# Gate matmuls of a recurrent layer: from two block-diagonal weights over the whole array to one head per half of the array's rows

## The chip, the cores and the metric

The kernel runs on one core of one Trainium2 chip. The metric is the device time of one execution in microseconds (us), lowest is best. TensorE (PE in the profile) does the matmuls, VectorE (DVE) and ScalarE (ACT) the elementwise work, GpSimd (POOL) and SyncE (SP) mostly issue DMAs.

## The reference, cut to what matters

One pre-norm layer over 2048 prompt positions and 128 sample positions (8 streams of 16), model width 1024. RMSNorm, one input projection, two branches (S5 and RG-LRU), a gated merge, an output projection, a final RMSNorm. The change is in the RG-LRU branch, whose two gates are block-diagonal: 16 heads of 64 channels, each with its own 64x64 weight per gate.

```python
xc, conv_new = causal_conv(u_b, conv_buf, conv_w, conv_b)
xh = xc.reshape(bt, L, LRU_HEADS, LRU_HEAD_DIM)            # 16 heads of 64
r = sigmoid(einsum('blhi,hij->blhj', xh, wa) + ba)         # recurrence gate
i = sigmoid(einsum('blhi,hij->blhj', xh, wx) + bx)         # input gate
log_a = -8.0 * r * softplus(-lam)
a = exp(log_a)
g = sqrt(max(-expm1(2 * log_a), 0)) * (i * xc)
h_t = a_t * h_{t-1} + g_t
y_b = h * silu(z_b);  p_b = y_b @ w_pb
```

## The kernel before, in words

Channels lie on the 128 partitions and positions along the free dimension. The 2176 positions are cut into five tiles `n`: four of 512 columns and one of 128. The 1024 recurrent channels are cut into eight blocks `b` of 128 channels, so a block holds two heads of 64.

Every fp32 product is made of three fp16 passes: weight and data are each split into a high and a low half, and the passes are high x high, high x low, low x high (`gemm`). A projection (`proj`) of one block and tile is 8 x 3 = 24 such matmuls.

The stage of the change is "stage B", a loop over `b`. It has an order written out by hand, and each engine runs its instructions in that order:

1. For each `n`: PE does the projection of the branch input (`proj`), and from `n` = 2 on the gate matmuls of tile `n-2` (`gates_pe`). ACT copies the projection out (`ub`), DVE does the width-4 convolution into `xc` (four instructions), ACT applies the two Tanh of the gates of `n-2` (`gates_a`, tiles `pt` and `q`), ACT rounds `xc` to the fp16 high half (`conv_hi`, tile `xs`), ACT does Exp and Tanh of `gates_b`, DVE makes the low half (`conv_lo`), DVE multiplies (`gates_c`).
2. `split_bd` splits the next block's gate weights (tile `wbs`).
3. For `n` = 0 and 1: the projection of the branch's SiLU gate, with the gate matmuls of tiles 3 and 4 behind it, then `gates_a`, `silu_tile` (tile `sz`), `gates_b`, `gates_c` of these.
4. The next streamed weight is split on ACT and DVE (`ws.step`, tile `wsp`). ACT loads the table for Sqrt and does `root_tile` for all five tiles; DVE then does product, scan and output product for each tile (`scan_tile`, `y_hi`, `y_lo`), while ACT goes back to the Tanh table for the last three `silu_tile`.

PSUM has four buffers `mm` for the projections and two each of `a` and `b` for the gates, 512 fp32 columns each. A projection can start only when the one four back has been read. After stage B comes stage P4B (gate B, projection B, and the S5 branch interleaved in it), where the same four `mm` buffers go round.

Before the change one block's weights are `[128, gate, 128]`: for each gate a 128x128 matrix with the two heads' 64x64 blocks on its diagonal and zeros elsewhere. `gates_pe` issues three 128x128 matmuls of 512 columns for the recurrence gate into buffer `a`, then three for the input gate into `b`; the output rows are the 128 channels in order, so one Tanh of 128 partitions evacuates each gate.

Of the kernel before, what the change touches and what calls it, by code (L numbers as in the profile page):

```python
# [17 lines left out]
P = 128  # L18
D = 1024
# [10 lines left out]
# column starts of the combined input projection  # L30
C_UA, C_ZA, C_UB, C_ZB, C_GA, C_GB = 0, 512, 1024, 2048, 3072, 4096

# power-of-two scales of the fp16 (high, low) parts
# [9 lines left out]
# per-pair parameter record of the S5 branch (float32 words per partition)  # L43
# [5 lines left out]
def build(tc, I, O):  # L49
# [30 lines left out]
    with ExitStack() as es:  # L80
# [45 lines left out]
        class Stream:  # L126
# [18 lines left out]
            def step(self):  # L145
                """splits the next block and starts the load two further on."""
                while self.nl < min(self.ns + 2, len(self.jobs)):
                    self.load()
                self.split()
                while self.nl < min(self.ns + 2, len(self.jobs)):  # L150
                    self.load()
# [6 lines left out]
        def rstd(r, ss, t):  # L158
            """r = -2 / sqrt(ss / D + eps): the table's root, then one Newton step."""
            act(r, ss, AF.Sqrt, scale=1.0 / D, bias=epsb)  # L160
            ts(t, ss, 1.0 / D, EPS, MUL, ADD)
            V.reciprocal(out=r, in_=r)
            if r.shape[1] == 1:
                stt(t, r, t, r, MUL, MUL)
            else:
                tt(t, t, r, MUL)
                tt(t, t, r, MUL)
            stt(r, t, -3.0, r, ADD, MUL)
# [3 lines left out]
        def gemm(p, W, rhs, nk):  # L172
            """p += the three passes of (Wh + Wl)^T (xh + xl) over nk blocks of the contraction."""
            for k in range(nk):
                xh, xl = rhs(k)
                PE.matmul(p, lhsT=W[:, k, 0], rhs=xh, start=(k == 0), stop=False)  # L176
                PE.matmul(p, lhsT=W[:, k, 0], rhs=xl, start=False, stop=False)  # L177
                PE.matmul(p, lhsT=W[:, k, 1], rhs=xh, start=False, stop=(k == nk - 1))  # L178
# [11 lines left out]
        wbdt = cp.tile([P, 2, 2, P], F32, name="wbd")  # L190
        G.memset(wbdt, 0.0)
        wbd = [wbdt[:, i] for i in range(2)]

        def load_bd(b):
            r = wbd[b % 2]
            for i, k in enumerate(("lru_wa", "lru_wx")):
                for h in range(2):
                    SP.dma_start(out=r[64 * h:64 * h + 64, i, 64 * h:64 * h + 64], in_=I[k][0, 2 * b + h])
# [27 lines left out]
        # =====================================================================  # L226
        # RMSNorm of the input, its transpose, and the S5 input projection
        # =====================================================================
# [5 lines left out]
        with ExitStack() as p1x:  # L234
# [84 lines left out]
            def params():  # L319
# [37 lines left out]
                def gma(out, a, f, b):  # L357
                    """out = f * a + b"""
                    gts(out, a, f)
                    gtt(out, out, b, ADD)  # L360

                def pexp(out, x):
                    """exp by range reduction and a polynomial."""
                    n, r, a, t = nt(), nt(), nt(), nt()
                    gts(x, x, -87.0, 88.0, MAX, MIN)
                    gts(n, x, 1.0 / math.log(2.0), MAGIC, MUL, ADD)
                    gts(n, n, -MAGIC, op0=ADD)
                    gma(t, n, -0.693359375, x)
                    gma(r, n, 2.12194440e-4, t)
                    G.memset(a, 1.0 / 5040)  # L370
                    for f in (720, 120, 24, 6, 2, 1, 1):
                        gtt(a, a, r, MUL)
                        gts(a, a, 1.0 / f, op0=ADD)
                    gts(n, n, 127.0, 8388608.0, ADD, MUL)
                    G.tensor_copy(out=r.bitcast(I32), in_=n)
                    gtt(out, a, r, MUL)
# [10 lines left out]
                def reduce_(a, k):  # L387
                    """a minus its nearest multiple of two pi."""
# [39 lines left out]
                # lambda_bar and the input coefficient (lambda_bar - 1) / lambda  # L428
# [11 lines left out]
                # lambda_bar^16 in polar form  # L440
                gtt(l16[:, 0], m16, cs[:, 1], MUL)
                gtt(l16[:, 1], m16, sn[:, 1], MUL)
                # parameters stacked by (re, im) over the partitions, one column per group
# [26 lines left out]
                # B_bar = coefficient * B, and i * B_bar  # L470
# [9 lines left out]
                # phasors exp(i 16 theta c), c = 0..127  # L480
# [73 lines left out]
            # the first tile: transposed as its rows arrive, all eight banks at once  # L554
# [68 lines left out]
        # =====================================================================  # L623
        # generic slots for everything that follows
        # =====================================================================
# [14 lines left out]
        # recurrent and convolution states, tails of both  # L640
# [24 lines left out]
        def split_bd(b):  # L665
            w = gt([P, 2, 2, P], F16, name="wbs")
            wsplit(w, wbd[b % 2], 2)
            wbs[b] = w
# [4 lines left out]
        def conv_tile(b, n, p):  # L673
            """evacuates the projection, applies the causal convolution, splits the result."""
# [36 lines left out]
        def gates_pe(b, n):  # L711
            w = TILES[n][1]
            xc, xs = st[b, n]
            out = []
            for i, tag in enumerate("ab"):
                p = ps(tag)[:, :w]
                gemm(p, wbs[b][:, i:i + 1], lambda k: (xs[:, 0], xs[:, 1]), 1)
                out.append(p)
            return out

        def gates_a(b, n, pr, pi):
            xc = st[b, n][0]
            pt, q = wt(n, name="pt"), wt(n, name="q")
            act(pt, pr, AF.Tanh, scale=0.5 / WS, bias=HB[:, b:b + 1])
            act(q, pi, AF.Tanh, scale=0.5 / WS, bias=HB[:, 8 + b:9 + b])
# [155 lines left out]
        def s5_mats(q):  # L881
# [9 lines left out]
            # wb[j, g, h, t] = lambda^(15 - 8j - t) B_bar, wc[j, g, h, t] = C lambda^(8j + t + 1)  # L891
# [21 lines left out]
        def s5_pe1(q):  # L913
# [10 lines left out]
            # lag kernels K[0..15] of both groups  # L924
# [147 lines left out]
        def out_states2():  # L1072
            # S5: lambda_bar^16 h0 + v for the samples, the last chunk state for the prompt
# [304 lines left out]
```

## Time and profile before

| | |
|---|---|
| time, median of 3 timed runs | 1560.04 us (1558.78 to 1561.81) |
| span of the profiled execution, first to last instruction | 1562.1 us |
| the profiled execution's own time | no other than its span; the span lies 2.1 us above the median |
| instructions | 22054 |
| PE busy | 1509.9 us, 97% of the span |
| DVE busy | 886.2 us, 57% |
| ACT busy | 632.9 us, 41% |
| TensorE clock granted, mean | 0.995 of full |

A busy PE is not a PE at its peak: a matmul's record lasts until its results are out, so records overlap. The distance from one start to the next is the pace. The same holds for ACT and DVE records, whose ends overlap the next start a little.

### The profile page before, as it was taken

The page shows a single profiled execution, that of the slowest core. Times are in us where ns is not written, and L with a number is a line of the kernel's source. Part 1 is how long each engine was busy: PE and PEld are TensorE (multiplying, and loading weights), DVE is VectorE, ACT ScalarE, POOL GpSimd, SP SyncE. Part 2 cuts the span into 40 slices and gives each one's busy share as a digit, 9 for nine tenths or more (in the row PEclk, how much of TensorE's full clock was granted, in tenths as well). Part 3 has the DMA queues.
Part 4 walks back from the last instruction along what each step waited for, and adds up shares of the span by engine and source line. Part 5 has one row for each costly group of instructions (what it writes and reads, how often), then busy time and mean ns, then how long its engine had stood idle before and what let it go on. Part 6 is the DMA issues. An engine that isn't in the chain of part 4 may idle for free.

```text
span 1562.1 us, 22054 instructions
## 1 busy us (share of the span) xinstructions
PE 1509.9 (97%) x8552; PEld 759.2 (49%) x8552; DVE 886.2 (57%) x1841; ACT 632.9 (41%) x1204; POOL 170.5 (11%) x344
## 2 busy tenths in 40 slices
PE   7999999999999999999999999979999999999998
PEld 4544444444444445555555554435444444444444
DVE  6557688878888775566655411864623320473333
ACT  7544465456545624444444311742322221242222
POOL 0780000000000003122222210000000000220000
PEclk9999999999999999999999999989999999999999
DMA  8298010101000123323333222231211210352331
GB/s 205 92 98 198 14 29 16 29 14 29 16 27 14 41 71 91 100 84 89 104 90 105 61 62 70 78 103 50 91 50 49 78 49 14 109 168 94 108 108 68
DMA packets 133458, 115.99 MB, mean 74 GB/s; under 512 B 35146, under 2 KB 112602, under 8 KB 132840
## 3 DMA queue, kind: packets, MB, share of 16 engines
q1 hardware_dynamic: 126056, 95.65, 23.4%
q0 software_dynamic: 7296, 18.92, 3.8%
q8 instruction: 67, 1.10, 0.3%
q14 instruction: 39, 0.32, 0.1%
HBM read 83.01 MB, written 31.53 MB: 73 GB/s over the span
## 4 chain that ended last, share of the span: by engine, by line
PE 68%; DVE 18%; ACT 8%; issue 2%; DMA 2%; POOL 1%; SPq 0%; POOLq 0%; DVEq 0%; ACTq 0%
PE ps_mm L176 17%; PE ps_mm L177 17%; PE ps_mm L178 17%; PE ps_mm L1333 4%; PE ps_mm L1334 4%; PE ps_mm L1332 4%; DVE xc L66 3%; DVE q L752 2%; ACT L75 1%; DVE sz L54 1%; ACT yh L75 1%; DVE q L54 1%; DVE wo L66 1%; ACT wsp L75 1%; PE ps_a L932 1%
## 5 line engine op out<-in xcount | busy, mean ns | idle before, releaser
L176 PE MATMUL ps_mm<-hT,wsp 128*128 128x512 f16 (+1 forms) x1440 | 486.2, 347 | 2.2 <-DVE qz L66 1.9
L177 PE MATMUL ps_mm<-hT,wsp 128*128 128x512 f16 (+1 forms) x1440 | 486.7, 347 | 0.0
L178 PE MATMUL ps_mm<-hT,wsp 128*128 128x512 f16 (+1 forms) x1440 | 485.7, 347 | 0.0
L177 PEld LDWEIGHTS <-wsp 128*128 128x128 f16 x2000 | 195.9, 98 | 198.6 <-issue 14.6
L176 PEld LDWEIGHTS <-wsp 128*128 128x128 f16 x2000 | 195.9, 98 | 191.6 <-issue 6.5
L178 PEld LDWEIGHTS <-wsp 128*128 128x128 f16 x2000 | 195.9, 98 | 189.5 <-issue 1.1
L66 DVE SCALAR_TENSOR_TENSOR wsp<-wraw,wsp 128x1024 f16<-128x1024 f32 (+1 forms) x56 | 62.0, 1108 | 111.2 <-ACT wsp L75 110.5
L176 PE MATMUL ps_mm<-y,wsp 128*128 128x512 f16 (+1 forms) x320 | 108.2, 347 | 0.0
L178 PE MATMUL ps_mm<-y,wsp 128*128 128x512 f16 (+1 forms) x320 | 108.2, 347 | 0.0
L177 PE MATMUL ps_mm<-y,wsp 128*128 128x512 f16 (+1 forms) x320 | 108.2, 347 | 0.0
L1333 PE MATMUL ps_mm<-wo,m 128*128 128x512 f16 (+2 forms) x280 | 104.1, 373 | 0.2 <-DVE wo L66 0.2
L1332 PE MATMUL ps_mm<-wo,m 128*128 128x512 f16 (+2 forms) x280 | 104.1, 373 | 0.0
L1334 PE MATMUL ps_mm<-wo,m 128*128 128x512 f16 (+2 forms) x280 | 104.0, 373 | 0.0
L1125 POOL DMA_DIRECT2D mbD<-gb x40 | 22.0, 551 | 663.6 <-DVE gb L66 663.5
L66 DVE SCALAR_TENSOR_TENSOR xc<-ub,PC,xc 128x512 f32<-128x512 f32 (+1 forms) x120 | 80.6, 672 | 4.2
L75 ACT ACTIVATE ga<-ps_mm 128x512 f32<-128x512 f32 (+1 forms) x40 | 21.2, 532 | 123.5 <-PE ps_mm L178 123.5
L75 ACT ACTIVATE gb<-ps_mm 128x512 f32<-128x512 f32 (+1 forms) x40 | 21.2, 530 | 121.0 <-PE ps_mm L178 90.8
L66 DVE SCALAR_TENSOR_TENSOR ga<-ga,ps_mm 128x512 f32<-128x512 f32 (+1 forms) x40 | 24.1, 602 | 79.2 <-PE ps_mm L178 78.8
L75 ACT ACTIVATE jk<-xo 128x512 f16<-128x512 f32 (+2 forms) x35 | 21.6, 617 | 109.5 <-DVE xo L66 109.5
L66 DVE SCALAR_TENSOR_TENSOR xo<-ps_mm,xo 128x512 f32<-128x512 f32 (+2 forms) x35 | 23.6, 675 | 71.0 <-PE ps_mm L1334 71.0
L75 ACT ACTIVATE y<-sz 128x512 f16<-128x512 f32 (+1 forms) x40 | 22.6, 566 | 94.3 <-DVE sz L54 94.3
L75 ACT ACTIVATE xs<-xc 128x512 f16<-128x512 f32 (+1 forms) x40 | 22.6, 566 | 90.7 <-DVE xc L66 90.7
(260 smaller groups left out, 2345.1 us busy)
## 6 DMA issues: line engine op xcount, KB each, us to landing
wraw<-w_in SPq DMA_DIRECT2D x40, 512.0 KB, 4.0
xt<-x_prompt SPq DMA_DIRECT2D x16, 512.0 KB, 4.2
mbD<-gb POOLq DMA_DIRECT2D x32, 256.0 KB, 2.3
ya<-yDp SPq DMA_DIRECT2D x32, 256.0 KB, 4.5
mb<-mbD SPq DMA_DIRECT2D x32, 256.0 KB, 4.2
xo<-x_prompt SPq DMA_DIRECT2D x16, 512.0 KB, 4.5
o_y_prompt<-xo SPq DMA_DIRECT2D x16, 512.0 KB, 2.9
uD<-uE POOLq DMA_DIRECT2D x4, 1088.0 KB, 11.4
```

Source lines behind the costliest of these rows:

```text
L54: V.tensor_tensor(out=out, in0=a, in1=b, op=op)
L66: V.scalar_tensor_tensor(out=out, in0=a, scalar=s, in1=b, op0=op0, op1=op1)
L75: S.activation(out=out, in_=a, func=f, **kw)
L176: PE.matmul(p, lhsT=W[:, k, 0], rhs=xh, start=(k == 0), stop=False)
L177: PE.matmul(p, lhsT=W[:, k, 0], rhs=xl, start=False, stop=False)
L178: PE.matmul(p, lhsT=W[:, k, 1], rhs=xh, start=False, stop=(k == nk - 1))
L752: V.tensor_tensor_scan(out=q, data0=a, data1=q, initial=0.0 if n == 0 else prev[:, w - 1:w], op0=MUL, op1=ADD)
L932: PE.matmul(o[:, 16 + P * j:16 + P * j + w], lhsT=lb, rhs=d["wc"][:, j, g].rearrange("p (h t) -> p t h", t=8)[:, 0:w // 16], start=True, s ...
L1125: G.dma_start(out=mbD[m, :, t0:t0 + w], in_=g)
L1332: PE.matmul(p, lhsT=lh[0], rhs=wo[:, k, 0, c], start=(k == 0), stop=False)
L1333: PE.matmul(p, lhsT=lh[0], rhs=wo[:, k, 1, c], start=False, stop=False)
L1334: PE.matmul(p, lhsT=lh[1], rhs=wo[:, k, 0, c], start=False, stop=(k == KB - 1))
```

## The change

The two heads of a block no longer sit on the diagonal of a 128x128 matrix. Head `h` keeps its rows, the partitions `64*h` to `64*h+63`, and its two 64x64 gate blocks lie side by side in the columns; for head 0 the recurrence gate comes first, for head 1 the input gate (`c = 64 * (i ^ h)`). A matmul therefore contracts over 64 rows, yields 128 output rows, and there is one PSUM buffer for each head in place of one for each gate: `a` holds head 0 (recurrence gate in rows 0 to 63, input gate in 64 to 127), `b` holds head 1 (input gate in rows 0 to 63, recurrence gate in 64 to 127). The three passes are issued in turn for the two heads: six matmuls as before, each on half of the array's rows. The zero fill of the weight tile goes away, and the split of the weights handles 128 columns in place of 256. `gates_a` evacuates by halves: four Tanh of 64 partitions in place of two of 128, because each gate's rows now come from both buffers. The rest of the diff removes comments.

```diff
-        wbdt = cp.tile([P, 2, 2, P], F32, name="wbd")
-        G.memset(wbdt, 0.0)
+        wbdt = cp.tile([P, 2, P], F32, name="wbd")
         wbd = [wbdt[:, i] for i in range(2)]
         def load_bd(b):
             r = wbd[b % 2]
             for i, k in enumerate(("lru_wa", "lru_wx")):
                 for h in range(2):
-                    SP.dma_start(out=r[64 * h:64 * h + 64, i, 64 * h:64 * h + 64], in_=I[k][0, 2 * b + h])
+                    c = 64 * (i ^ h)
+                    SP.dma_start(out=r[64 * h:64 * h + 64, c:c + 64], in_=I[k][0, 2 * b + h])
...
         def split_bd(b):
-            w = gt([P, 2, 2, P], F16, name="wbs")
-            wsplit(w, wbd[b % 2], 2)
+            w = gt([P, 2, P], F16, name="wbs")
+            scopy(w[:, 0], wbd[b % 2], WS)
+            stt(w[:, 1], wbd[b % 2], WS, w[:, 0], MUL, SUB)
             wbs[b] = w
...
         def gates_pe(b, n):
             w = TILES[n][1]
             xc, xs = st[b, n]
-            out = []
-            for i, tag in enumerate("ab"):
-                p = ps(tag)[:, :w]
-                gemm(p, wbs[b][:, i:i + 1], lambda k: (xs[:, 0], xs[:, 1]), 1)
-                out.append(p)
+            out = [ps(tag)[:, :w] for tag in "ab"]
+            for i, (l, r) in enumerate(((0, 0), (0, 1), (1, 0))):
+                for h in range(2):
+                    c = slice(64 * h, 64 * h + 64)
+                    PE.matmul(out[h], lhsT=wbs[b][c, l], rhs=xs[c, r], start=(i == 0), stop=(i == 2))
             return out
 
-        def gates_a(b, n, pr, pi):
+        def gates_a(b, n, p0, p1):
             xc = st[b, n][0]
             pt, q = wt(n, name="pt"), wt(n, name="q")
-            act(pt, pr, AF.Tanh, scale=0.5 / WS, bias=HB[:, b:b + 1])
-            act(q, pi, AF.Tanh, scale=0.5 / WS, bias=HB[:, 8 + b:9 + b])
+            lo, hi = slice(0, 64), slice(64, P)
+            for dst, d, src, c, o in ((pt, lo, p0, lo, 0), (pt, hi, p1, hi, 0), (q, lo, p0, hi, 8), (q, hi, p1, lo, 8)):
+                act(dst[d], src[c], AF.Tanh, scale=0.5 / WS, bias=HB[d, o + b:o + b + 1])
             ts(pt, pt, 1.0, 0.0, ADD, MAX)
             st[b, n] = (xc, pt, q)
```

## Rows read from the trace of the kernel before

**Rows 1.** Page, busy us, share of the span, instructions.
```profile
PE 1509.9 (97%) x8552; PEld 759.2 (49%) x8552; DVE 886.2 (57%) x1841; ACT 632.9 (41%) x1204; POOL 170.5 (11%) x344
```

**Rows 2.** Windows: one block of stage B, a part of it, stage P4B.
```profile
core 0: us, PE busy (x) PEld busy (x) DVE busy (x) ACT busy (x) POOL busy (x), PEclk, DMA share, GB/s
399.70:452.10 52.40, 50.26 (x272) 24.18 (x271) 42.85 (x80) 28.69 (x53) 0.00 (x0) 1.00 0.08 22
...
420.60:434.90 14.30, 14.30 (x72) 6.70 (x71) 11.32 (x24) 13.41 (x25) 0.00 (x0) 1.00 0.08 24
...
585.00:920.00 335.00, 335.00 (x2299) 187.04 (x2297) 184.39 (x503) 137.56 (x308) 76.75 (x130) 1.00 0.30 89
```

**Rows 3.** Waits of PE, 125 to 560 us: total, times, longest.
```profile
PE ps_a L176 <- ACT xs L75: 9.2, 14, 0.7
PE ps_a L177 <- DVE xs L54: 5.8, 14, 0.5
```

**Rows 4.** Chain that ended last, block 5: start, us, what.
```profile
415.22 0.38 PE ps_a L177
...
428.32 0.37 ACT pt L75
```

**Rows 5.** Timeline of ACT, block 5 (start, us, instruction, idle before).
```profile
419.25 0.63 ACT L75 ACTIVATE xs<-xc 128x512 f16<-128x512 f32 x1 [1.89 <-DVE xc L66]
...
421.31 0.68 ACT L75 ACTIVATE pt<-ps_a,HB 128x512 f32<-128x512 f32 x1
421.88 0.68 ACT L75 ACTIVATE q<-ps_b,HB 128x512 f32<-128x512 f32 x1
423.07 0.31 ACT L75 ACTIVATE xs<-xc 128x128 f16<-128x128 f32 x1 [0.51 <-DVE xc L66]
...
424.17 0.72 ACT L75 ACTIVATE pt<-pt,SPL 128x512 f32<-128x512 f32 x1
424.80 0.40 ACT L75 ACTIVATE wbs<-wbd 128x256 f16<-128x256 f32 x1
425.10 0.67 ACT L75 ACTIVATE pt<-ps_a,HB 128x512 f32<-128x512 f32 x1
...
427.47 0.72 ACT L75 ACTIVATE pt<-pt,SPL 128x512 f32<-128x512 f32 x1
428.32 0.37 ACT L75 ACTIVATE pt<-ps_a,HB 128x128 f32<-128x128 f32 x1
428.59 0.36 ACT L75 ACTIVATE q<-ps_b,HB 128x128 f32<-128x128 f32 x1
428.84 0.60 ACT L75 ACTIVATE sz<-ps_mm 128x512 f32<-128x512 f32 x1
```

**Rows 6.** Timeline of DVE, block 5: the first scan's product, the third SiLU.
```profile
433.08 0.69 DVE L54 TENSOR_TENSOR q<-q,pt 128x512 f32<-128x512 f32 x1 [0.72 <-ACT pt L75]
...
441.01 0.69 DVE L66 SCALAR_TENSOR_TENSOR sz<-sz,ps_mm 128x512 f32<-128x512 f32 x1 [2.60 <-ACT sz L75]
```

**Rows 7.** Timeline of ACT in P4B: four copies of 64 partitions out of PSUM.
```profile
579.00 1.14 ACT L75 ACTIVATE v<-ps_a 64x136 f32<-64x136 f32 x4 [0.49 <-PE ps_a L965]
```

**Rows 8.** Timeline of ACT, block 0: gates of its last tile.
```profile
166.27 0.37 ACT L75 ACTIVATE pt<-ps_a,HB 128x128 f32<-128x128 f32 x1 [2.81 <-PE ps_a L178]
...
166.78 0.60 ACT L75 ACTIVATE sz<-ps_mm 128x512 f32<-128x512 f32 x1
```

**Rows 9.** Timelines of DVE and PE where stage B ends.
```profile
553.85 0.68 DVE L66 SCALAR_TENSOR_TENSOR sz<-sz,ps_mm 128x512 f32<-128x512 f32 x1
...
555.23 0.38 PE L176 MATMUL ps_mm<-hT,wsp 128*128 128x512 f16 x1
```

**Rows 10.** Timeline of PE: gate matmuls of one tile, back to back.
```profile
415.87 0.38 PE L177 MATMUL ps_b<-xs,wbs 128*128 128x512 f16 x1
416.08 0.38 PE L178 MATMUL ps_b<-xs,wbs 128*128 128x512 f16 x1
```

**Rows 11.** Timeline of PE in P4B: from 32-column to whole-array matmuls.
```profile
571.94 1.03 PE L932 MATMUL ps_a<-wc,par 128*32 128x128 f32 x7
572.90 0.39 PE L176 MATMUL ps_mm<-y,wsp 128*128 128x512 f16 x1
```

## Prediction, on record before the result

> **What bounds the kernel now.** I began with the page: PE is busy for 97% of the span, which invites the sentence "PE is the bound, so PE time saved is time won" [rows 1]. That is an average over stages, so I asked next for windows. In P4B, PE is busy for all of 335 us; in one block of stage B it is busy for 50.26 of 52.40 us, with DVE at 42.85 and ACT at 28.69 [rows 2]. The 2.1 us that are missing in each block have names: PE waits for `xs`, the split convolution output, first for ACT's high half and then for DVE's low half, 15.0 us over the stage [rows 3]. An engine that waits for its followers isn't the bound there, so I read the chain of the stage. In block 5 it enters PE at 415.22 and leaves it at 428.32, to ACT's first Tanh of the last gate tile [rows 4]. That is 13.1 us of PE in a period of 52.4; the other 39 us of each period are DVE and ACT: convolution, split, roots, scans, output products. Only matmuls issued between these two times can shorten a block.
>
> Then the question is what is second there. The timeline of ACT shows it: from 423.07 on ACT runs one instruction after another up to the roots; in the 14.3 us around them it is busy for 13.41 [rows 2, 5]. The Tanh of 428.32 follows a Tanh of 427.47; at the pace that such a one has (424.17 to 424.80, 0.63 us) ACT came free at 428.10 [rows 5]. So PE is ahead of ACT in setting this time by 0.22 us and no more. What starts behind it, the roots, is waited for: DVE's first scan product stood 0.72 us for its root [rows 6].
>
> **The change part by part.** *PE.* Six matmuls of a tile start 0.21 to 0.22 us apart [rows 10]. If the matmuls of two heads run side by side, a 512-column tile saves three of them, 0.65 us. Over 32 such tiles, and 8 of a quarter of the columns, that is 20.8 + 1.3 = 22 us. No row shows two matmuls side by side in the two halves of the rows, so the bounds are 0 and 0.65 us a tile; I take 0.65, since it has little weight below: in a block only two groups lie between the two times of the chain, 1.30 us, and ACT is 0.22 us behind.
>
> A switch of the array's partition may cost something too. The row that is nearest: the seventh 32-column matmul's record ends at 571.94 + 1.03 = 572.97, and the next whole-array matmul starts at 572.90, so no gap is seen at that switch [rows 11]. The sum takes 0. The upper bound is the overlap of two neighbours lost, 0.38 - 0.21 = 0.17 us a switch, two switches a group [rows 10]. The Trainium skill ("TensorEngine Tiling (Array Packing)", Tiling Modes, Key Properties) speaks against the change here: changing the tiling mode drains TensorE. By that rule half of the saving goes, and the time would be 0.7 us longer (the third rival); the rows of the 32-column switch do not bear it out. For the pairing only the skill has a statement ("TensorE: Matmul & The Clock Gate", Part 3): matmuls in different row groups run concurrently; by it the saving is the 0.65 us that I take, and no row here shows it.
>
> *ACT.* Two Tanh become four of half the partitions. Does half the height cost half? The nearest row says no: four copies of 64x136 out of PSUM took 1.14 us, 0.285 us each, while whole-height Tanh of 128 columns start 0.27 us apart (428.32, 428.59) [rows 5, 7]. Time goes by columns. So a half-height Tanh of 512 columns is priced as a whole one, 0.57 us (421.31 to 421.88), and a tile costs 2 x 0.57 = 1.14 us more, the last tile 0.52 us more (428.32 to 428.84 for two) [rows 5]. The bounds are 0 (half height, half price) and this.
>
> How much of it is on the path, in a block like block 5 [rows 5]:
> - tiles 0 and 1: behind them ACT waits for the convolution, 1.89 us and more; 1.14 fits in. 0.
> - tile 2: its second Tanh lets ACT free at 421.88 + 0.57 = 422.45, the next instruction starts at 423.07. 0.62 is hidden, 0.52 us is not.
> - the split of the gate weights has 128 columns less: (0.57 - 0.27) / 3 = 0.10 us less. DVE's half of it is not waited for.
> - tile 3: ACT is back to back. 1.14 us.
> - tile 4: 0.52 us, less the 0.22 us that ACT stood for PE. 0.30 us.
>
> Sum: 0.52 - 0.10 + 1.14 + 0.30 = 1.86 us later at the roots. What is late next: the Sqrt table load, the roots, the first scan, and by the chain all of the scans, the last SiLU and the next block's convolution. Is there slack to take it up? DVE waits 2.60 us for the third SiLU [rows 6], but that SiLU stands behind the return to the Tanh table, which stands behind the second output product of DVE itself; it moves along. So each period grows from 52.4 to 54.3 us.
>
> *The ends.* Block 0 is different: ACT stands 2.81 us for PE before its last gate tile [rows 8], so PE's saving of two groups counts, -1.30 us, and the two extra Tanh cost 0.52: -0.78 us. Blocks 1 to 6 give 6 x 1.86 = 11.2. In block 7 there is no gate weight to split, so 1.96 there: DVE and ACT reach the end of the stage 12.4 us late. PE doesn't wait for all of it: the first matmul that needs their work is the projection at 555.23, which takes the PSUM buffer that DVE finished reading at 553.85 + 0.68 = 554.53; 0.70 us of slack [rows 9]. PE would come there on its own 10.4 - 1.3 = 9.1 us late, so it waits, and leaves stage B 12.4 - 0.7 = 11.7 us late. P4B has PE full [rows 2], so this goes through to the end.
>
> *At nothing:* the weight loads (as many DMAs, a block ahead), the zero fill at the program's start, the HBM traffic, the DVE operations on `pt` and `q` (they wait for the last Tanh, which in tiles 0 and 1 ends before the convolution does).
>
> Sum on the profiled execution: 1562.1 + 11.7 = 1573.8 us. Its span is 2.1 us above the median of the runs shown, so the forecast is 1571.7 us, 0.75% slower. A measurement of this kernel can tell about 0.2%, 3.1 us, from no change.
>
> **The rivals.**
> 1. *PE is the bound all through stage B.* Then 22 us come off: 1538. For it: 97% busy. Against it: the named waits and a chain that is on PE for a quarter of a period [rows 3, 4]. 0.04.
> 2. *Half height, half price on ACT.* Then ACT gains nothing and loses nothing, each block shortens by the 0.22 us of slack and the 0.10 us of the split, block 0 by 1.3, the end by 0.7: 1556, faster. It decides at a pace of about 0.38 us for 64x512: there the extra 4 x 0.38 - 1.14 = 0.38 us a tile, 1.46 times in a block (tiles 3 and 4), just pays for the 0.32 us, and block 0's gain for the rest. Against it: 0.285 us for 136 columns [rows 7]. 0.05.
> 3. *Every switch drains PE* (the rule above). Block 0 keeps 0.62 of its 1.30 us: 1572.4. 0.12.
> 4. *The heads don't run side by side.* The change doesn't do what it says, PE saves nothing, block 0 gives +0.52 in place of -0.78: 1573.0. Nothing in the rows excludes it; it would hardly show in the time. 0.12.
> 5. *The delay is taken up within the block*, in DVE's 2.60 us [rows 6]. Then blocks 1 to 6 give nothing and what stays is -0.78 + 1.96 - 0.70: 1560.5, no change. Against it: both sides of that wait hang on the same chain. 0.07.
>
> **How the numbers follow.** My own case has 0.60, and its time is the forecast. Cases 3 and 4 lie beside it, so slower holds 0.84, no change 0.07, faster 0.09. The range: with a half-height pace of 0.53 to 0.60 us for 0.57, the block's sum moves by -0.4 to +0.3 us, seven times, -2.8 to +2; if tile 2 were hidden too, -3.6 at most; no pairing adds 1.3. I take 1566 to 1577, which leaves out cases 1, 2 and 5, 0.16.
>
> **What the profile after would show.** Four Tanh of 64 partitions in each tile, each near 0.68 us long and 0.57 apart; ACT some 49 us busier by its records (64 x 0.68 + 16 x 0.36). Gate matmuls of 64 rows whose starts come in pairs, or 0.21 us apart if case 4 holds. The period of a block near 54.3 us, the wait of PE for ACT's `xs` at two places in a block grown from 0.7 to about 2 us, the wait of ACT for PE before the last gate tile gone. P4B and all behind it unchanged in length and shifted by 11.7 us. The forecast is wrong if a 64x512 Tanh has a pace well below 0.57 us, or if ACT still waits for PE between tile 3 and the roots; and too low if the longer waits of PE bring its granted clock to the lower level.

## The result, and the profile after

The changed kernel takes 1585.83 us (median of 4 runs, 1585.14 to 1587.13) against 1559.95 us for the kernel before in the same measurement (4 runs, 1558.78 to 1561.81). The ratio is 1.0168, with a 95% interval of 1.0154 to 1.0182: 1.7% slower. The forecast was 1571.7 us, in a range of 1566 to 1577. The direction and the place were right, the size was half of what came.

The page of the changed kernel, in the columns of [rows 1]:

```profile
PE 1508.3 (95%) x8552; PEld 748.6 (47%) x8552; DVE 890.6 (56%) x1841; ACT 687.7 (43%) x1284; POOL 170.6 (11%) x343
```

PE's and DVE's busy times hardly move; ACT has 80 instructions and 54.8 us more. Windows of one block of stage B and of stage P4B, as in [rows 2]:

```profile
391.30:447.23 55.93, 48.81 (x264) 21.98 (x263) 42.91 (x79) 35.52 (x62) 0.00 (x0) 0.97 0.07 21
607.00:942.00 335.00, 334.17 (x2275) 185.75 (x2273) 184.63 (x507) 138.39 (x307) 76.49 (x129) 1.00 0.30 90
```

A block has grown from 52.4 to 55.9 us, DVE's work in it is the same, and ACT has 6.8 us more. P4B is as full as before: it is shifted, not changed. From one Sqrt table load to the next, six periods of the kernel before are 52.41 us on average and the seventh is 52.96. After the change the six are 55.84 to 55.93, 20.75 us longer together, and the seventh is 56.74, 3.78 longer; the first load comes 1.20 us earlier. So the last load comes 20.75 + 3.78 - 1.20 = 23.3 us later, and this is what the spans differ by too (1585.4 and 1562.1).

The timeline of ACT in the changed kernel's block 5 shows where a period grows; it answers to [rows 5] (`sz` is the SiLU's Tanh, `a` the Exp of `gates_b`):

```profile
433.91 0.67 ACT L75 ACTIVATE pt<-ps_a,HB 64x512 f32<-64x512 f32 x1
434.60 0.68 ACT L75 ACTIVATE pt<-ps_b,HB 64x512 f32<-64x512 f32 x1
...
436.71 0.31 ACT L75 ACTIVATE xs<-xc 128x128 f16<-128x128 f32 x1
...
438.50 0.67 ACT L75 ACTIVATE pt<-ps_a,HB 64x512 f32<-64x512 f32 x1
...
440.59 0.68 ACT L75 ACTIVATE q<-ps_b,HB 64x512 f32<-64x512 f32 x1
441.29 0.60 ACT L75 ACTIVATE sz<-ps_mm 128x512 f32<-128x512 f32 x1
441.91 0.72 ACT L75 ACTIVATE a<-pt,SPL 128x512 f32<-128x512 f32 x1
...
443.29 0.35 ACT L75 ACTIVATE pt<-ps_a,HB 64x128 f32<-64x128 f32 x1
...
444.80 0.60 ACT L75 ACTIVATE sz<-ps_mm 128x512 f32<-128x512 f32 x1
```

And the lines of block 5 before the change that the next paragraph needs besides [rows 5]:

```profile
426.24 0.59 ACT L75 ACTIVATE sz<-ps_mm 128x512 f32<-128x512 f32 x1
426.71 0.72 ACT L75 ACTIVATE a<-pt,SPL 128x512 f32<-128x512 f32 x1
...
429.31 0.41 ACT L75 ACTIVATE a<-pt,SPL 128x128 f32<-128x128 f32 x1
```

Read the starts, not the lengths. A record is 0.68 us long before and after, but before the next Tanh started 0.57 us later [rows 5], and here it starts 0.70 us later. The four Tanh of tile 2 take 2.80 us, and the idle 0.51 us in front of `xs` is gone. Slot by slot, the changed kernel against the kernel before: first Tanh of tile 2 to `xs` 2.80 for 1.76, +1.04; `xs` to the Tanh of tile 3 1.79 for 2.03, -0.24; tile 3's Tanh to its `sz` 2.79 for 1.14, +1.65; the Exp behind that `sz` +0.15; from there to tile 4's Tanh -0.23, the wait for PE that is gone; tile 4's Tanh to `sz` 1.51 for 0.52, +0.99; the next Exp +0.16. The sum is 3.5 us, the growth of the period.

PE's side is small. The timeline of PE, one gate tile between two projections, which answers to [rows 10]:

```profile
435.01 0.38 PE L178 MATMUL ps_mm<-hT,wsp 128*128 128x512 f16 x1
435.32 0.39 PE L721 MATMUL ps_a<-xs,wbs 64*128 64x512 f16 x1
435.33 0.39 PE L721 MATMUL ps_b<-xs,wbs 64*128 64x512 f16 x1
...
435.77 0.38 PE L721 MATMUL ps_b<-xs,wbs 64*128 64x512 f16 x1
436.08 0.39 PE L176 MATMUL ps_mm<-hT,wsp 128*128 128x512 f16 x1
```

The two heads of a pair start 0.01 us apart here, so they do run side by side. Each switch between whole and half array shows as a step of 0.31 us where 0.215 is usual, 0.1 us more. From the last projection matmul to the next one it is 1.07 us, where seven steps of 0.215 would be 1.5: 0.44 us saved a tile.

PE's saving turns into longer waits. PE's waits of the changed kernel, 125 to 600 us, against [rows 3]:

```profile
PE ps_mm L176 <- DVE sz L66: 19.6, 13, 2.1
PE ps_a L721 <- ACT xs L75: 15.5, 9, 1.8
```

And the chain of waits in block 5, which was on PE for 13.1 us [rows 4], goes over DVE and ACT alone from 422 to 446 us; a few of its lines (start, us, what):

```profile
431.84 0.63 ACT xs L75
...
434.60 0.68 ACT pt L75
```

### The profile page after: what moved, and what is told of

Its sections match the earlier page's. It is cut to its first block, busy times and chain, and to the rows that moved or that the text cites. A ratio compares the mean times of both kernels' runs of the same rounds, so it can differ in the third digit from the quotient of the medians.

```text
span 1585.4 us, 22133 instructions
## 1 busy us (share of the span) xinstructions
PE 1508.3 (95%) x8552; PEld 748.6 (47%) x8552; DVE 890.6 (56%) x1841; ACT 687.7 (43%) x1284; POOL 170.6 (11%) x343
## 4 chain that ended last, share of the span: by engine, by line
PE 55%; DVE 15%; ACT 13%; issue 2%; DMA 1%; SPq 0%; ACTq 0%; DVEq 0%; POOL 0%
PE ps_mm L176 14%; PE ps_mm L178 13%; PE ps_mm L177 13%; DVE xc L66 4%; PE ps_mm L1337 4%; PE ps_mm L1336 4%; PE ps_mm L1338 4%; ACT pt L75 3%; DVE q L756 2%; ACT q L75 2%; ACT a L75 1%; DVE sz L54 1%; ACT L75 1%; DVE q L54 1%; ACT yh L75 1%
## 5 line engine op out<-in xcount | busy, mean ns | idle before, releaser
L66 DVE SCALAR_TENSOR_TENSOR gb<-gb,ps_mm 128x512 f32<-128x512 f32 (+1 forms) x40 | 24.0, 602 | 62.0 <-PE ps_mm L178 62.0
```

Of the source, the lines that this page charges most:

```text
L66: V.scalar_tensor_tensor(out=out, in0=a, scalar=s, in1=b, op0=op0, op1=op1)
```

## The experiments

The theory was that ACT's four Tanh carry the whole loss, because half-height instructions follow each other at 0.70 us where whole ones do at 0.57, and that the paired matmuls by themselves are a small gain. The rival was that something on TensorE carries it, or part of it: the switches, or the granted clock, which fell from 0.995 to 0.988 over the whole run. Inside the first theory it was open what makes the pace 0.70. Each expectation explains its own letters. The first four and the next four kernels ran on chips where the kernel before took 1564.05 and 1563.54 us, so ratios are compared, each against the kernel before on the same chip.

**1. The paired matmuls with two Tanh.** After's matmuls; `gates_a` applies two Tanh of 128 partitions, one to each head's buffer, which mixes up the rows of the two gates.

```diff
-            lo, hi = slice(0, 64), slice(64, P)
-            for dst, d, src, c, o in (...):
-                act(dst[d], src[c], AF.Tanh, scale=0.5 / WS, bias=HB[d, o + b:o + b + 1])
+            act(pt, p0, AF.Tanh, scale=0.5 / WS, bias=HB[:, b:b + 1])
+            act(q, p1, AF.Tanh, scale=0.5 / WS, bias=HB[:, 8 + b:9 + b])
```

> The matmul half of the change alone: pairs of 64-row matmuls as in the changed kernel, but two whole-height Tanh as before (pt from head 0's buffer, q from head 1's, so the rows of the two gates are mixed up and the output is not the reference's; the work per engine is what is wanted). Theory A (all of the loss is ScalarE's four Tanh, matmul pairing is harmless and nearly worthless): ACT loses its extra 2 x 0.57 us a tile, each block gives back the 0.22 us for which ACT stood for PE and the 0.10 us of the smaller weight split, block 0 about 1 us: 1556 us (1554 to 1559). Theory B (half-array matmuls cost something: switches of the array, a clock that falls, PSUM buffers given back late): 1565 us or more, with a block's period above 53 us. Theory C (PE is the bound of the stage, and pairing is worth its 0.4 us a tile or more): 1545 us or less.

Measured: 1565.46 us, ratio 1.0013 (1.0003 to 1.0023). The loss is gone, but the gain isn't there. The windows of three of its blocks say why (granted clock: third number from the end):

```profile
329.68:381.73 52.05, 48.94 (x274) 22.53 (x273) 42.72 (x79) 28.53 (x51) 0.00 (x0) 1.00 0.08 22
381.73:433.83 52.10, 48.48 (x272) 22.33 (x270) 42.71 (x79) 28.53 (x52) 0.00 (x0) 1.00 0.08 22
433.83:487.04 53.21, 49.56 (x269) 22.57 (x268) 42.79 (x79) 28.60 (x51) 0.00 (x0) 0.97 0.07 20
```

Blocks of one run take some 52.05 or 53.2 us (three of each among the six), and the long ones have the lower clock. The timeline of PE in the long block:

```profile
469.45 0.37 PE L721 MATMUL ps_a<-xs,wbs 64*128 64x512 f16 x1 [1.62 <-ACT xs L75]
...
470.32 0.37 PE L721 MATMUL ps_a<-xs,wbs 64*128 64x512 f16 x1 [0.48 <-DVE xs L54]
...
471.26 0.63 PE L177 MATMUL ps_mm<-hT,wsp 128*128 128x512 f16 x1
471.69 0.63 PE L178 MATMUL ps_mm<-hT,wsp 128*128 128x512 f16 x1
```

Behind two waits, 1.62 and 0.48 us, the matmuls follow each other 0.43 us apart, twice the usual step: 1.2 GHz in place of 2.4. It lasts until the matmul that starts at 474.49, some 3.6 us. With two Tanh the chain is on PE there, so PE's delay lengthens the block by 1.16 us. The waits alone don't set it off: in the block from 381.73 PE waits as long (2.9 us for ACT's `xs`, 0.8 for DVE's; 2.8 and 0.8 in the long one), and its clock stays at 1.00. This was not in the forecast's sum, which had the pairing as 0.3 us a block of gain if ACT costs nothing (rival 2).

**2. The four Tanh alone.** The kernel before with its whole-array matmuls; only `gates_a` is cut, both gates of the low half first.

```diff
-            act(pt, pr, AF.Tanh, scale=0.5 / WS, bias=HB[:, b:b + 1])
-            act(q, pi, AF.Tanh, scale=0.5 / WS, bias=HB[:, 8 + b:9 + b])
+            lo, hi = slice(0, 64), slice(64, P)
+            for d in (lo, hi):
+                for dst, src, o in ((pt, pr, 0), (q, pi, 8)):
+                    act(dst[d], src[d], AF.Tanh, scale=0.5 / WS, bias=HB[d, o + b:o + b + 1])
```

> The evacuation half of the change alone: block-diagonal 128x128 matmuls as before, each gate's Tanh cut into two of 64 partitions, in the order pt low, q low, pt high, q high, so that the first and second, and the third and fourth, read and write the same partitions. Theory A: all of the loss comes back, and a little more, since PE no longer helps block 0 (about 1.3 us) and the weight split is whole (0.1 us a block): 1588 us (1586 to 1591), period of a block 56.0 us, if half-height instructions never overlap (0.70 us apart). Theory A2 (the overlap is lost only where the partitions written change from one instruction to the next): starts 0.57, 0.70, 0.57, 0.70 us apart, 0.26 us a tile less than the above, about 2.5 tiles in each of seven blocks, 1583 us. Theory B: 1560 to 1563 us.

Measured: 1589.08 us, ratio 1.0159 (1.0138 to 1.0179), periods of 55.6 us. Most of the loss comes without any change on PE. That the two ratios lie so close is in part chance: from the first Sqrt load to the last this kernel takes 22.3 us more than the kernel before, the changed kernel 24.5, and the profiled execution has the rest ahead of the first load, where PE waited 5.2 us for a DMA (3.1 in the kernel before, none in the changed one). And the pace is not 0.70 throughout, as the timeline of ACT shows:

```profile
443.38 0.68 ACT L75 ACTIVATE pt<-ps_a,HB 64x512 f32<-64x512 f32 x1
443.96 0.67 ACT L75 ACTIVATE q<-ps_b,HB 64x512 f32<-64x512 f32 x1
444.64 0.68 ACT L75 ACTIVATE pt<-ps_a,HB 64x512 f32<-64x512 f32 x1
445.23 0.67 ACT L75 ACTIVATE q<-ps_b,HB 64x512 f32<-64x512 f32 x1
445.91 0.60 ACT L75 ACTIVATE sz<-ps_mm 128x512 f32<-128x512 f32 x1
446.54 0.72 ACT L75 ACTIVATE a<-pt,SPL 128x512 f32<-128x512 f32 x1
```

Two in the same half are 0.58 us apart; a step from one half to the other is 0.68. So it isn't the half height as such.

**3. The changed kernel with its Tanh ordered by output half:** `pt` low, `q` low, `q` high, `pt` high.

```diff
-... in ((pt, lo, p0, lo, 0), (pt, hi, p1, hi, 0), (q, lo, p0, hi, 8), (q, hi, p1, lo, 8)):
+... in ((pt, lo, p0, lo, 0), (q, lo, p0, hi, 8), (q, hi, p1, lo, 8), (pt, hi, p1, hi, 0)):
```

> The changed kernel with its four Tanh in another order: pt low, q low, q high, pt high, so the output stays the reference's. First and second write the same partitions but read other ones, second and third change both, third and fourth write the same. If a change of the partitions written is what parts two instructions (A2): starts 0.57, 0.70, 0.57 us apart and 1581 us. If reading from other partitions than one writes to, or half height as such, is what does it: 0.70 us three times and 1585.8 us as the changed kernel (1584 to 1587).

Measured: 1594.59 us, ratio 1.0202 (1.0184 to 1.0219), slower than the changed kernel. The timeline of ACT:

```profile
440.13 0.67 ACT L75 ACTIVATE pt<-ps_a,HB 64x512 f32<-64x512 f32 x1
440.81 0.69 ACT L75 ACTIVATE q<-ps_a,HB 64x512 f32<-64x512 f32 x1
441.51 0.68 ACT L75 ACTIVATE q<-ps_b,HB 64x512 f32<-64x512 f32 x1
...
443.38 0.72 ACT L75 ACTIVATE a<-pt,SPL 128x512 f32<-128x512 f32 x1 [0.16 <-DVE pt L72]
```

All steps are 0.68 to 0.70, also between two that write the same half but read different ones. The output half alone isn't the condition. And `pt` is now complete only with the last Tanh, so DVE's step on it is late and ACT waits for it, 0.16 us of the 0.6 us by which a block is longer than in the changed kernel. Part of the rest is lost overlap behind the tile, which now ends on the upper half of PSUM: the `ub` copies start 0.75 us after the instruction ahead of them, in the changed kernel 0.63.

**4. Four Tanh of whole height and half the columns,** on the kernel before.

```diff
-            act(pt, pr, AF.Tanh, scale=0.5 / WS, bias=HB[:, b:b + 1])
-            act(q, pi, AF.Tanh, scale=0.5 / WS, bias=HB[:, 8 + b:9 + b])
+            h = TILES[n][1] // 2
+            for dst, src, o in ((pt, pr, 0), (q, pi, 8)):
+                for c in (slice(0, h), slice(h, 2 * h)):
+                    act(dst[:, c], src[:, c], AF.Tanh, scale=0.5 / WS, bias=HB[:, o + b:o + b + 1])
```

> The kernel before with each gate's Tanh cut into two of 128 partitions and 256 columns: four instructions a tile as in the changed kernel, but whole height. If the loss is the fixed cost of two more instructions that still overlap (0.27 us at 128 columns and 0.10 us for each 128 more: 0.37 us apart), a tile costs 4 x 0.37 - 1.14 = 0.34 us more, hidden in tile 2; with 0.14 us for the last tile some 0.5 us a block: 1563.5 us (1562 to 1566). If any cut of one output tile into two instructions ends the overlap (0.48 us apart), 0.78 us a tile: 1570 us.

Measured: 1565.73 us, ratio 1.0020 (1.0008 to 1.0033). Two instructions stand in one line of its timeline of ACT:

```profile
426.16 0.82 ACT L75 ACTIVATE pt<-ps_a,HB 128x256 f32<-128x256 f32 x2
426.87 0.83 ACT L75 ACTIVATE q<-ps_b,HB 128x256 f32<-128x256 f32 x2
```

0.71 us for two halves by columns, against 0.57 for the whole: four instructions of all partitions cost 0.28 us a tile more, where four of half the partitions cost 1.65. The number of instructions is a small part of the loss.

**A theory for the pace.** Put together: where nothing else holds it, an instruction of ACT starts some 0.1 us before the one ahead has ended when its accesses begin at the same partition, and doesn't when the half of its input or of its output differs. (Something else holds the second instruction of `gates_b`: it overwrites the `pt` that the first reads, its record carries a wait for ACT's own semaphore, and it starts behind the end of the first at whole height too, 426.71 and 427.47 in the kernel before.) The changed kernel's order, (input, output) = (low, low), (high, high), (high, low), (low, high), changes at least one at every step, and so would any other order of its four Tanh, since the four pairs all differ. That the output counts by itself is seen behind tile 3: from `q` (low, high; 440.59) to `sz` (low, low; 441.29), which reads no bias, it is 0.70 us as well. The next run keeps half height and takes the change of half away; experiment 7 turns the order of experiment 2 round.

**5. Four half-height Tanh, all on partitions 0 to 63.** On the kernel before; the low half is evaluated twice, and POOL fills the upper half with zeros, so the gates of the second head are left out.

```diff
-            act(pt, pr, AF.Tanh, scale=0.5 / WS, bias=HB[:, b:b + 1])
-            act(q, pi, AF.Tanh, scale=0.5 / WS, bias=HB[:, 8 + b:9 + b])
+            lo, hi = slice(0, 64), slice(64, P)
+            for t in (pt, q):
+                G.memset(t[hi], 0.0)
+            for k in range(2):
+                for dst, src, o in ((pt, pr, 0), (q, pi, 8)):
+                    act(dst[lo], src[lo], AF.Tanh, scale=0.5 / WS, bias=HB[lo, o + b:o + b + 1])
```

> The kernel before with four half-height Tanh a tile that all read and write partitions 0 to 63 (pt, q, pt, q); the upper half of pt and q is set to zero by POOL, so the gates of the second head are left out. Theory A3 (an instruction of ScalarE starts before its predecessor ends only if its first partition, read from PSUM, read from SBUF and written, is that of the last such access; half height as such costs nothing more): starts 0.57 us apart, each block grows by 0.52 + 1.14 + 0.30 = 1.96 us as the prediction had it, seven of them less 0.7 at the end, with block 0: +13 us, a ratio of 1.008 (1.006 to 1.010), period 54.4 us. Rival (half height as such parts them): 0.70 us apart, period 55.8 us, ratio 1.016.

Measured: 1578.18 us, ratio 1.0094 (1.0077 to 1.0111), periods of 54.1 to 54.6 us. The timeline of ACT:

```profile
433.79 0.67 ACT L75 ACTIVATE pt<-ps_a,HB 64x512 f32<-64x512 f32 x1
434.36 0.67 ACT L75 ACTIVATE q<-ps_b,HB 64x512 f32<-64x512 f32 x1
434.93 0.67 ACT L75 ACTIVATE pt<-ps_a,HB 64x512 f32<-64x512 f32 x1
```

0.57 us each time: the pace that the forecast had taken, at half height. And the six periods are 54.3 us on average, where the sum gives 54.4 (the forecast's 54.3 without the 0.10 us of the smaller split, which this kernel doesn't have). With this pace the sum comes out.

**6. Experiment 1, with PE kept busy.** Six matmuls of 512 columns whose results the gates overwrite stand ahead of the gates of tiles 0 and 2.

```diff
+            if n in (0, 2):
+                for i in range(6):
+                    PE.matmul(out[i % 2], lhsT=wbs[b][:, 0], rhs=hT[0][:, i, 0], start=True, stop=True)
```

> The matmul half alone (two whole-height Tanh, gates mixed up) with six idle matmuls of 512 columns put into the gates' own PSUM buffers ahead of the gate matmuls of tiles 0 and 2, where PE waits for the split convolution output anyway; their results are overwritten. Theory D (pairing by itself gained its 0.3 us a block, and lost it again because longer waits of PE brought its granted clock down to 1.2 GHz for some 4 us of a block): the granted clock is 1.00 in every block, periods of 52.05 us in all of them in place of 52.05 and 53.2 mixed, and the time is 0.2% below the kernel before (ratio 0.996 to 0.999). Rival (the clock was not it; the pairs or their switches cost it): the ratio stays at 1.001 or above.

Measured: 1559.75 us, ratio 0.9977 (0.9967 to 0.9986). All periods of the main stretch are 52.0 to 52.1 us, as in this window of one of them:

```profile
323.84:375.89 52.05, 50.95 (x284) 23.37 (x282) 42.73 (x79) 28.53 (x51) 0.00 (x0) 1.00 0.08 22
```

The clock stays at 1.00, and matmuls that do nothing useful make the kernel 0.36% faster than experiment 1, some 5.6 us. The three long periods that are gone make 3.5 us of it. In the profiled executions the first Sqrt load comes 3.5 us earlier as well, where PE waited 1.2 us for a DMA (`rows` from `state_lru`) in place of 5.1, so not all of the gain can be put down to the clock. Against the period of the kernel before (on the first chip), the pairing and the smaller weight split are worth 52.41 - 52.05 = 0.36 us a block, when the clock holds.

**7. Experiment 2 with the high half first.**

```diff
-            for d in (lo, hi):
+            for d in (hi, lo):
```

> As the run with the evacuation half alone, but upper half first: pt high, q high, pt low, q low, so that the tile ends on partition 0, where the next whole-height instructions start. Theory A3: inside a tile as before (0.57, 0.69, 0.57), but lost overlaps come back behind it: 0.57 for 0.70 from the last Tanh to the next instruction, 0.47 for 0.63 from the SiLU's Tanh to the Exp, 0.63 for 0.75 from the gate's second Tanh to the copy of the next projection; one is newly lost, from that copy to the first Tanh. Period 55.0 us in place of 55.57, ratio 1.013 in place of 1.016. Rival (overlap depends on nothing but half height, or on the count of instructions): no change, 55.5 us or more.

Measured: 1583.71 us, ratio 1.0126 (1.0111 to 1.0142), periods of 54.9 us against 55.6 of experiment 2. The end of the group in the timeline of ACT:

```profile
440.40 0.67 ACT L75 ACTIVATE q<-ps_b,HB 64x512 f32<-64x512 f32 x1
440.97 0.58 ACT L75 ACTIVATE sz<-ps_mm 128x512 f32<-128x512 f32 x1
441.45 0.71 ACT L75 ACTIVATE a<-pt,SPL 128x512 f32<-128x512 f32 x1
```

These are the last Tanh of the low half and what follows. The last half is now the one where the next instruction begins: `q` to `sz` is 0.57 us where it was 0.68, and `sz` to the Exp is 0.48 where it was 0.63. The loss that was foreseen came too: from `ub` to the first Tanh, now of the upper half, it is 0.60 us for 0.48. The same work in another order of the halves is 0.3% faster.

**8. The changed kernel with the six idle matmuls** (the edit of 6).

> The changed kernel with the same idle matmuls. If the falls of PE's clock in the changed kernel (granted 0.94 to 1.00 by block) cost nothing because PE is not on the path there: clock near 1.00 in stage B, periods of 55.86 us as before, ratio 1.0165 (within 0.002 of the changed kernel). Rival (the clock is part of the 26 us): periods fall below 55.5 us and the ratio below 1.013.

Measured: 1588.62 us, ratio 1.0166 (1.0143 to 1.0189), as the changed kernel. The filling didn't hold the clock everywhere, and that makes the better test; the windows of two of its periods:

```profile
223.90:279.73 55.83, 52.71 (x284) 23.66 (x283) 42.90 (x79) 35.49 (x61) 0.00 (x0) 0.97 0.07 21
279.73:335.56 55.83, 51.34 (x284) 23.41 (x283) 42.90 (x79) 35.49 (x62) 0.00 (x0) 1.00 0.07 21
```

At 0.97 and at 1.00 a period is 55.83 us. In the changed kernel the clock falls too, but ACT sets the block, so it costs nothing.

**9. The chain's ACT work in another order,** on the kernel before, with its matmuls and its two Tanh. If the roots wait for ACT, work that they don't need can stand behind them. Both weight splits move behind the roots, and the first SiLU projection is issued ahead of the gates of tile 2, so that PE has work while `xs` is made.

```diff
                 p = proj(W, n)
+                if n == 4:
+                    W = ws.take(2 * b + 1)
+                    pz = proj(W, 0)
                 g = gates_pe(b, n - 2) if n >= 2 else None
...
-            if b + 1 < 8:
-                split_bd(b + 1)
...
-            ws.step()
             for n in range(NT):
                 root_tile(b, n)
+            ws.step_hi()
             for n in range(NT):
                 scan_tile(b, n)
+                if n == 1 and b + 1 < 8:
+                    w2 = gt([P, 2, 2, P], F16, name="wbs")
+                    scopy(w2[:, :, 0], wbd[(b + 1) % 2], WS)
...
                 if n == 1:
+                    ws.step_lo()
+                    if b + 1 < 8:
+                        stt(w2[:, :, 1], wbd[(b + 1) % 2], WS, w2[:, :, 0], MUL, SUB)
...
```

(`step_hi` and `step_lo` are the ACT half and the DVE half of `ws.step`.)

> A version drawn from the chain, on the kernel before (whole-height Tanh, block-diagonal matmuls, the reference's output): the instructions of ScalarE that stand between the last gate tiles and the roots are moved to where ScalarE waits for VectorE. The split of the next projection's weight goes behind the roots, that of the gate weights behind the first output product, their VectorE halves ahead of the third SiLU, where VectorE waits 2.6 us; and the first SiLU projection is issued ahead of the gate matmuls of tile 2, so that PE no longer stands for the split convolution output there. If the period is set by ScalarE in that stretch, each block loses 0.95 (projection weight) + 0.30 (gate weights) + 0.22 (the wait for PE) = 1.47 us, period 50.9 us, 7 blocks and block 0 with 1 us: 11 us, ratio 0.993 (0.991 to 0.995). If PE is the bound next at its 50.3 us busy and some waits, or VectorE's part of the splits is not hidden: periods of 51.5 us or more, ratio 0.996 or above.

Measured: 1549.58 us (5 runs, 1547.15 to 1549.98) against 1559.39 for the kernel before, ratio 0.9928 (0.9915 to 0.9942). The six periods are 50.9 us. A window of it, and its waits of PE from 125 to 560 us:

```profile
370.00:421.00 51.00, 50.15 (x272) 24.17 (x271) 42.67 (x79) 28.70 (x52) 0.00 (x0) 1.00 0.08 23
```

```profile
PE ps_a L193 <- DVE xs L54: 5.1, 14, 0.4
```

The 9.2 us that PE waited for `xs` of ACT [rows 3] are gone, ACT's busy time in a block is the same, and each block is 1.5 us shorter. The kernel beats both others without touching the matmuls. It moves several things at once; what each is worth was not tried apart.

## Why the prediction was right in its place and half in its size

**What bounds it: right.** The chain, on PE for 13.1 us of 52.4, and PE's waits named ACT and DVE for the rest of a block, and at the last gate tile ACT was ready only 0.22 us before PE. After the change the wait of ACT for PE ahead of the last gate tile is gone in block 5, the chain there is on ACT and DVE alone, and PE waits longer. Rival 1 (22 us faster) is out: PE saves its time and it is waited away. What the pairing and the smaller split can be worth in a block was 0.22 + 0.10 = 0.32 us by rival 2, and experiment 6 measured 0.36.

**The step that failed: "a half-height Tanh of 512 columns is priced as a whole one, 0.57 us".** It took 0.70 us, and 0.38 us for 128 columns in place of 0.26, because the half changes at every step; on one half alone it does take 0.57 (experiment 5). By the same sum, with 0.70: tile 2, 4 x 0.70 - 1.14 - 0.62 = 1.04 us (measured 1.04); tile 3, 4 x 0.70 - 1.14 = 1.66 (1.65); tile 4, 4 x 0.38 - 0.52 - 0.22 = 0.78 (0.99 - 0.23 = 0.76). With the split's -0.10 that is 3.4 us a block, where 3.5 came and 1.86 was forecast. Which tiles are hidden, what of tile 2 is, and that nothing later in the block takes the delay up (rival 5): all as forecast. Only the pace was wrong, and with it the bounds: a tile was to cost 1.14 us more at most and tile 3 cost 1.65, and the range's 0.53 to 0.60 did not hold 0.70. Three small terms that the sum didn't have make up the rest: the Exp behind each of the two `sz`, +0.15 and +0.16, and -0.14 between `xs` and the Tanh of tile 3.

The row that had it was in hand. Four copies of 64x136 took 1.14 us, 0.285 each [rows 7]. I compared this with the pace of a Tanh of another length, and concluded that time goes by columns. The view of costly groups by shape, of the kernel before, has the length of one such copy (count, busy us, mean ns of one):

```profile
L75 ACT ACTIVATE v<-ps_a 64x136 f32<-64x136 f32 x64 | 17.9, 279 | 1.6 <-PE ps_a L965 1.0
```

0.285 us apart, 0.279 us long: these copies do not overlap at all, while the whole-height Tanh do by 0.11 us [rows 5]. In the code they go from rows 0 to 63 and 64 to 127 of PSUM, in turn, to one half and then the other half of `v`: the half of the input changes at every step, as it does at two of the three steps in the changed `gates_a`. Pace against length of the same instruction would have shown the lost overlap; pace against another pace did not.

**Pairing: right, at two thirds of the size.** 0.44 us a tile for 0.65. The heads run side by side, so rival 4 is out; the Trainium skill's statement that matmuls in different row groups run concurrently ("TensorE: Matmul & The Clock Gate", Part 3) agrees. The switches cost 0.1 us each, two in a tile, where the sum had 0 and the bound 0.17. The Trainium skill's rule that a change of the tiling mode drains TensorE ("TensorEngine Tiling (Array Packing)", Key Properties) agrees in that a switch costs something, though the first 64-row matmul starts 0.07 us before the record ahead of it ends (435.32 against 435.01 + 0.38). As the chain isn't on PE, the switches moved the time by nothing that shows.

**The ends.** Up to the first Sqrt load the changed kernel gained 1.20 us, where the forecast had 0.78 for block 0. That isn't a confirmation: in the trace of before PE waited 3.1 us in that block for a DMA (`rows` from `state_lru`), which in the changed kernel's had landed in time, and there a new wait of 1.2 us for ACT's `q` appeared. Why the DMA was in time was not tried. Block 7 gave 3.78 for 1.96, the same pace as the others. The slack of PE at the end held. The timeline of PE, where it leaves stage B, for [rows 9]:

```profile
577.90 0.38 PE L176 MATMUL ps_mm<-hT,wsp 128*128 128x512 f16 x1 [2.11 <-DVE sz L66]
```

It is 22.7 us late where DVE and ACT are 23.3 late: 0.65 us taken up, for 0.70. P4B and what follows pass the delay on.

**From span to median.** Before, the profiled span lay 2.15 us above the median of 1559.95; after, it lies 0.4 us below. The 25.9 us between the medians are 23.3 of the traces and 2.6 of this, which no step of the sum speaks of: the forecast took the difference of 2.1 us to stay. In every execution that has both, the time is 1.7 to 2.0 us longer than the span (1587.13 and 1585.4 in the profiled one), so by an estimate from these the profiled execution of the kernel before took some 3.9 us more than the median, and that of the changed kernel 1.3. Of the 14.1 us by which the forecast was too low, 11.6 lie in the traces and the rest here.

**The clock.** The forecast named it as a way to come out too low. The clock did fall (0.97 in the block shown), but experiment 8 shows periods of 55.8 us at either clock. It costs only where PE is on the chain, as in experiment 1.

## What to carry to other kernels

Before you cut an instruction into halves of the partitions, compare in the trace the pace of a row of such halves with the length of one of them: equal numbers mean that the overlap is gone, and the cut is dearer than its columns say. Where the halves can't be avoided, order them so that the half changes as seldom as possible, and end on the one where the next instruction begins. When an engine that waits in every block is given less to do, look first at what it waits for: here another order of ACT's work, with one projection of PE moved along, was worth 0.7%, and the saved matmuls with the smaller split 0.2% at best.

## What the runs showed of the hardware that was not expected

**ACT's overlap hangs on the half that an instruction starts in.** Tanh of 512 columns that follow each other on ACT are 0.57 us apart at 0.68 us of length when the partitions where their accesses begin are the same, at whole and at half height (experiment 5), and 0.68 to 0.70 when the half of the input or of the output changes (the changed kernel, experiments 2 and 3). The Trainium skill ("ScalarE: Activation LUTs", What ACT_TABLE_LOAD costs) states that back-to-back instructions overlap by some 93 ns; the trace has 0.11 us between Tanh and 0.10 from `sz` to the Exp (440.97 + 0.58 against 441.45, experiment 7), and the runs add the condition. Starts at partitions 0 and 64 were tried, no others. The half seems to be remembered beyond the next instruction. In experiment 2 the `ub` copy, four instructions behind a Tanh of the high half, starts 0.75 us after the one ahead of it, and in experiment 7, where the last such Tanh is of the low half, 0.63. The timelines of ACT, experiment 2 and then 7:

```profile
432.24 0.72 ACT L75 ACTIVATE pt<-pt,SPL 128x512 f32<-128x512 f32 x1
432.99 0.60 ACT L75 ACTIVATE ub<-ps_mm 128x512 f32<-128x512 f32 x1
```

```profile
427.68 0.72 ACT L75 ACTIVATE pt<-pt,SPL 128x512 f32<-128x512 f32 x1
428.31 0.58 ACT L75 ACTIVATE ub<-ps_mm 128x512 f32<-128x512 f32 x1
```

The three instructions in between (`xs`, Exp, Tanh of `gates_b`) read and write SBUF alone, so it looks as if the last access to PSUM counts for the next one there, and the last one to SBUF for SBUF (the Exp behind `sz`, 0.63 against 0.48; ahead of both, the last read from SBUF is the bias of the last Tanh, from the upper half in experiment 2 and the lower in 7). That is argued from the rows; no run took the SBUF side by itself.

**Less work on PE can cost its clock.** In experiment 1 matmuls that were saved left waits of 1.62 and 0.48 us, the matmuls behind them ran at 1.2 GHz for some 3.6 us, and the block was 1.16 us longer; with idle matmuls in front (experiment 6) no block did. What exactly sets it off was not tried; another block of experiment 1 has as much waiting and keeps its clock.
